# RWKV-7 layer of a two-layer hybrid: k times (1 + ka(a−1)) and k times k_k are made where the keys are projected, and y's normalisation is given out later in the recurrence

## The chip, the cores and the metric

The kernel runs on one core of a Trainium2 chip. The metric is the device time of one execution in microseconds (us), the median of several. One execution was also taken by the hardware profiler; its page and trace are the profile spoken of below.

## The reference

A two-layer model works on 1104 columns of tokens: 16 meta tokens and a prompt of 1024, which form one sequence, and eight samples of eight tokens. The width is 1024. The first layer is a gated DeltaNet mixer, the second an RWKV-7 mixer with 16 heads of 64, and only the second is touched. Its core:

```python
def rwkv_mixer(xn, S0, shift_prev, mu, w_rkvz, ..., k_k, k_a, r_k, lnx_w, lnx_b, w_o):
    ...
    r, k, v, z = rkvz[0], rkvz[1], rkvz[2], rkvz[3]
    w = -jax.nn.softplus(-(w0 + jnp.tanh(xs[4] @ w1) @ w2)) - 0.5
    a = jax.nn.sigmoid(a0 + (xs[5] @ a1) @ a2)
    kk = l2norm((k * k_k).reshape(B, T, H, N))
    k = k * (1.0 + (a - 1.0) * k_a)
    decay = jnp.exp(-jnp.exp(w))
    ...
    def step(S, inp):
        r_t, k_t, v_t, d_t, kk_t, b_t = inp
        S = (S * d_t[:, :, None, :]
             + jnp.einsum('bhvk,bhk->bhv', S, -kk_t)[..., None] * b_t[:, :, None, :]
             + v_t[..., None] * k_t[:, :, None, :])
        return S, jnp.einsum('bhvk,bhk->bhv', S, r_t)
    ...
    y = (y - mean) * lax.rsqrt(var + GN_EPS) * lnx_w.reshape(H, N) + lnx_b.reshape(H, N)
    y = y + jnp.sum(r_h * k_h * r_k, -1, keepdims=True) * v_h
    y = y.reshape(B, T, D) * jax.nn.silu(z)
    return y @ w_o, S, xn[:, -1]
```

So the raw key k is used in two ways: times k_k it gives kk, and times 1 + (a − 1)·ka it gives the key of the recurrence. `omka` below is 1 − ka, so that the factor is ka·a + omka.

## The kernel before

The 1104 columns are cut into three segments (384, 384, 336), the 1024 channels into eight tiles of 128 partitions (two heads each). A pair of tile and segment is an item; the RWKV layer has 24 of them, n = 8 × segment + tile. Matmuls of the dense projections take the weight in two float32r parts: `whi` is ScalarE's rounded copy of the loaded `wraw`, `wlo` is GpSimd's difference (line 90). The inputs `xh`, `xa`, `xc` and `xl` of a projection are split likewise, and `mixs` is the token-shift mix before the split. `d` is the PSUM tile of such a projection.

The RWKV layer runs in stages, one after the other:

1. **Keys, decay and rate** (`keys_decay_rate`, lines 1112 to 1153; 1360 to 1480 us). For each of the eight tiles, the key projection of three segments (`project`: ScalarE copies each PSUM tile into `ev`, line 1109, and SyncE stores it to DRAM, line 1110), then two second halves of low-rank products (`flora`): for the decay a sigmoid, a scan along the columns on VectorE (line 1143) and a store; for the rate a a sigmoid and a store. The three results are slices of one DRAM tensor, `cakd` (c the scanned decay, a the rate, k the raw key).
2. **Projections of r, v and z** (24 calls of `project`), between which `rwkv_inverse` is called five times (1480 to 1862 us). It loads `sldcak` (line 1221), scales kk by k_k on ScalarE (line 1251), makes the normalised kk products (lines 1257 to 1264), and solves small triangular systems (`L`, `T1n`, `invT`, `mY`, `mU`, `fL`).
3. **The recurrence** (`wave`, lines 1820 and on; 1880 to 2310 us). Items start every second step and take six chunks of 64 columns, one a step, so that up to three items are in flight; there are 58 steps. A step's chain on TensorE and ScalarE: matmuls `rX` and `rY` from the last state, ScalarE's copy `X` (line 1466), matmuls of X with the inverse (`rX<-X,rTT`, `rS<-X,rTT`), ScalarE's two `UV` copies, matmuls `rS<-UV,BT` and `rY<-UV,G` in `step_inner`, and the new state.
4. The end of the output projection and the final norm (2310 to 2351 us).

Around the chain, each step also gives out work of other items. `rwkv_front` (line 1317) prepares the next item: it loads `fldcak` (c, a, k; 576 KB, one buffer) and `fldrv`, makes the decays `fDp` and `fiD`, makes the key of the recurrence on ScalarE (`k<-fldcak,omka,pcol`, line 1342) and VectorE (line 1343), and the tile BK from it; scores `fG`, transposes `fBT` copied to `BT`, and a `bonus` follow. `rwkv_finish` (line 1518) treats an item whose six chunks are done: bn_stats, the reciprocal root `grs` and the shift `gnm` on VectorE, then six ScalarE normalisations of y in place (line 1536), and behind a `yield` the transposes `yT` and VectorE's two products into `lz` (lines 1544 and 1545; the intermediate shares a one-buffer tile, tag `k2`, with the front's key), and behind another the split into `yh` and `yl` that feeds the output projection (`zo`, `do`). `fill` gives out dense matmuls between.

What sets the order: TensorE's order in the recurrence is that of the program. The other engines' queues are ordered by the scheduler's own simulation of the program at build time; everything under `issue_after(ins)` in a step stands behind the UV copies of that step on its engine. Every engine, and SyncE with its DMA issues, executes its queue in order. In `wave`, an item's `rwkv_finish` is begun at the end of the step of its last chunk, outside the reach of the next step's `issue_after`, so the normalisations stand where the scheduler puts them. `pre` is ScalarE's decayed state for the next step, given out by `step_old` right behind UV.

Of the kernel before, what the change touches and what calls it, by code (L numbers as in the profile page):

```python
# [35 lines left out]
class Builder:  # L36
# [867 lines left out]
    ev = None  # L904
# [193 lines left out]

    def project(self, m, k, x, dst, apart=False):

        nc, t = self.nc, self.t
        w = self.load_w(self.i["rwkv_w_rkvz"][0, m][:, 128 * k:128 * k + 128])
        ps = (self.dense(w, 128, *x, s, bufs=4) for s in range(2 if m == 3 else 3)) if apart else self.dense3(w, 128, *x)
        for (c0, n), p in zip(SEGS, ps):
            f = t(self.ev, [128, 384], "ev", 3)
            if m == 3:
                self.gate(f[:, 0:n], p[:, 0:n])
            else:
                nc.scalar.copy(f[:, 0:n], p[:, 0:n])
            nc.sync.dma_start(dst[k][:, c0:c0 + n], f[:, 0:n])  # L1110

    def keys_decay_rate(self, x, hh, hl):

        nc, t, i, col = self.nc, self.t, self.i, self.pcol
        with self.tc.tile_pool(name="lora", bufs=1, reuse_waits="tile") as pool:
            z = t(pool, [128, 8, 48], "zpad")
            nc.gpsimd.memset(z, 0.0)
            for d in (self.ad, self.rd, self.vd, self.zd, self.kd):
                nc.sync.dma_start(d[:, :, NT:1152].rearrange("k p n -> p k n"), z)
# [26 lines left out]
            def dst_a(k, s, p):  # L1146
                c0, n = SEGS[s]
                f = t(self.ev, [128, 384], "ev", 3)
                self.act(f[:, 0:n], p[:, 0:n], AF.Sigmoid, bias=col["rwkv_a0"][:, k:k + 1])
                nc.sync.dma_start(self.ad[k][:, c0:c0 + n], f[:, 0:n])  # L1150
            for k in range(8):
                self.project(1, k, x, self.kd, k in (0,))
                self.lora_second(0, k, hh, w2, dst_w)
                self.lora_second(1, k, hl, w2, dst_a)
# [4 lines left out]
    def rwkv_masks(self, ap, first=False):  # L1159
# [42 lines left out]
        self.omka = t(ap, [128, 8], "omka")  # L1202
        nc.vector.tensor_scalar(self.omka, self.pcol["rwkv_k_a"], -1.0, 1.0, op0=ALU.mult, op1=ALU.add)

    def rwkv_open(self):
        self.cakd, self.rvd, self.zd = (self.dram([8, 128, n, 1152], m) for n, m in ((3, "cakd"), (2, "rvd"), (1, "zd")))
        self.csd, self.ad, self.kd = (self.cakd[:, :, x] for x in range(3))
        self.rd, self.vd = (self.rvd[:, :, x] for x in range(2))
        self.zd = self.zd[:, :, 0]
        self.ttd, self.abd = self.dram([5, 128, 1920], "ttd"), self.dram([24, 128, 768], "abd")  # L1210

    def rwkv_load(self, n, pool, tag, names):
# [4 lines left out]
        for g in names:  # L1217
            d = {"cak": self.cakd, "rv": self.rvd}[g]
            y = 1 if tag == "s" else 0
            x = t(pool, [128, y + len(g), 384], tag + "ld" + g, 1 if g == "cak" and tag == "f" else 2)  # L1220
# [18 lines left out]
    def rwkv_inverse(self, b, pool):  # L1239
# [4 lines left out]
        for q, n in enumerate(items):  # L1244
# [6 lines left out]
            self.act(kk, kk, AF.Identity, scale=self.pcol["rwkv_k_k"][:, p:p + 1])  # L1251
# [65 lines left out]
    def rwkv_front(self, p, s):  # L1317
# [11 lines left out]
        ld = self.rwkv_load(P.n, fp, "f", ("cak", "rv"))  # L1329
# [11 lines left out]
        k2 = t(fp, [128, 384], "k2", 1)  # L1341
        self.act(k2, ld["a"], AF.Identity, scale=pc("rwkv_k_a"), bias=self.omka[:, p:p + 1])
        nc.vector.tensor_tensor(k2, k2, ld["k"], op=ALU.mult)

        nc.vector.tensor_tensor(BK[:, :, 0, :], c6(k2), c6(iD), op=ALU.mult)
# [4 lines left out]
        nc.vector.scalar_tensor_tensor(pr, ld["r"], pc("rwkv_r_k"), k2, op0=ALU.mult, op1=ALU.mult)  # L1350
# [167 lines left out]
    def rwkv_finish(self, p, s, P):  # L1518
# [15 lines left out]
        nc.vector.scalar_tensor_tensor(nm, mv[:, :, 0], -1.0, rs, op0=ALU.mult, op1=ALU.mult)  # L1534
        for q in range(6):
            self.act(y(q), y(q), AF.Identity, scale=rs[:, q:q + 1], bias=nm[:, q:q + 1])
        yield
# [280 lines left out]
    def wave(self, zin, stay, last, pool):  # L1818
# [63 lines left out]
        for tau in range(-3, 55):  # L1882
# [12 lines left out]
            with self.tc.issue_after(ins) if W else ExitStack():  # L1895
                if W:
                    self.step_old(W)
                for f in begun:
                    next(f)
# [54 lines left out]
```

## Time and profile before

| | us |
|---|---|
| median of 3 runs (2350.22 to 2353.13) | 2350.88 |
| the profiled execution | 2353.39 |
| its span, first to last instruction | 2351.5 |
| TensorE busy in it | 2157.2 (92%) |
| VectorE busy | 1570.0 (67%) |
| ScalarE busy | 1298.2 (55%) |
| GpSimd busy | 922.5 (39%) |
| mean granted TensorE clock | 0.969 |

In the profile PE is TensorE's matmul side and PEld its weight loads, DVE VectorE, ACT ScalarE, POOL GpSimd and SP SyncE, which issues the DMAs. A row of a view of waits reads "waiting engine, tile and line, <- engine, tile and line waited for: us in total, times, longest". A row of a timeline reads "start, duration, engine, line, operation, out<-in, shapes, count", with the idle time before it and its releaser in brackets. A row of groups ends with "count | busy us, mean ns of one | idle us before, and what ended it". Several like instructions in a row of one engine are shown as one row with their count.

### The profile page before, as it was taken

What the parts mean: (1) busy time and instruction counts of PE and PEld (TensorE: products, weight loads), DVE (VectorE), ACT (ScalarE), POOL (GpSimd) and SP (SyncE); (2) the same over time, 40 slices, a digit from 0 to 9 for tenths busy, and PEclk for the clock granted to TensorE, in tenths of its full rate; (3) what the DMA queues carried; (4) which work ended last, traced back from release to release, by engine and by line L of the source; (5) the groups of instructions that cost most, each with busy time, mean ns of one, the idle gap of its engine ahead of it and who ended that gap; (6) DMA issues with size and microseconds to landing.
All of it is one profiled execution on the core that took longest, in us unless ns stands there. A gap on an engine that the chain in (4) does not pass through costs nothing. (4 is left out here: it accounts for less than half of the span.)

```text
span 2351.5 us, 55207 instructions
## 1 busy us (share of the span) xinstructions
PE 2157.2 (92%) x20452; PEld 1959.8 (83%) x20452; DVE 1570.0 (67%) x4176; ACT 1298.2 (55%) x3690; POOL 922.5 (39%) x1267
## 2 busy tenths in 40 slices
PE   6989999989999999999999999898888898899986
PEld 5878988889898989888999999787777876778775
DVE  6768668685857677684335842679879365667754
ACT  5455555465655645556333655746555355677763
POOL 3435334343435343444131532545324333344443
PEclk9999999999999999999999999999999999999998
DMA  4324332423333333336153154654543655577654
GB/s 114 107 67 113 84 86 79 109 63 101 91 97 96 88 101 82 93 82 206 51 147 106 47 149 167 181 167 128 172 123 94 187 141 141 174 219 229 208 167 136
DMA packets 431704, 293.36 MB, mean 125 GB/s; under 512 B 146906, under 2 KB 414283, under 8 KB 431435
## 3 DMA queue, kind: packets, MB, share of 16 engines
q1 hardware_dynamic: 431434, 289.83, 42.8%
q8 instruction: 161, 2.64, 0.5%
q14 instruction: 109, 0.89, 0.1%
HBM read 202.74 MB, written 87.00 MB: 123 GB/s over the span
## 5 line engine op out<-in xcount | busy, mean ns | idle before, releaser
L90 POOL TENSOR_TENSOR wlo<-wraw,whi 128x512 fp32r<-128x512 f32 (+2 forms) x252 | 330.9, 1315 | 370.1 <-ACT whi L86 354.6
L76 PE MATMUL d<-xc,whi 128*128 128x384 f32 (+2 forms) x910 | 258.6, 340 | 9.3 <-POOL xc L90 3.5
L86 ACT CAST whi<-wraw 128x512 fp32r<-128x512 f32 (+2 forms) x252 | 151.7, 603 | 128.1 <-PE dq L76 50.6
L415 DVE SCALAR_TENSOR_TENSOR cvy<-raw,cw,cvy 128x408 f32<-128x408 f32 (+2 forms) x288 | 178.5, 633 | 16.9 <-ACT cvy L62 15.1
L76 PEld LDWEIGHTS d<-xc,whi 128*128 128x128 f32 (+1 forms) x910 | 166.5, 189 | 15.9 <-POOL xc L90 3.8
L453 DVE TENSOR_TENSOR invT<-invT,invtmp 72x31 f32<-72x31 f32 (+31 forms) x403 | 171.5, 426 | 6.5
L451 DVE TENSOR_TENSOR invtmp<-invA,invT 72x31 f32<-72x31 f32 (+31 forms) x403 | 165.3, 410 | 12.5 <-DMA invA<-ltd 5.4
L76 PE MATMUL dz<-xc,whi 128*128 128x384 f32 (+1 forms) x480 | 149.7, 343 | 0.0
L76 PE MATMUL dv<-xc,whi 128*128 128x384 f32 (+1 forms) x480 | 146.7, 334 | 0.0
L76 PE MATMUL d<-xc,wlo 128*128 128x384 f32 (+2 forms) x428 | 141.5, 340 | 0.9 <-POOL wlo L90 0.8
L76 PE MATMUL d<-xa,whi 128*128 128x384 f32 (+3 forms) x450 | 139.3, 344 | 3.3 <-DVE xa L90 1.8
L815 POOL TENSOR_SCALAR Sb<-Sb,eglb 128x128 f32<-128x128 f32 x128 | 81.0, 651 | 89.4 <-DMA Sb<-in_state_gdn 44.4
L76 PE MATMUL dz<-xa,whi 128*128 128x384 f32 (+1 forms) x288 | 100.5, 349 | 0.0
L76 PE MATMUL dv<-xa,whi 128*128 128x384 f32 (+1 forms) x288 | 100.1, 347 | 0.1
L76 PEld LDWEIGHTS dz<-xc,whi 128*128 128x128 f32 x480 | 89.8, 192 | 0.8
L76 PEld LDWEIGHTS d<-xa,whi 128*128 128x128 f32 (+1 forms) x450 | 84.0, 191 | 7.5 <-DVE xa L90 2.4
L76 PE MATMUL d<-xa,wlo 128*128 128x384 f32 (+3 forms) x252 | 85.9, 342 | 3.8 <-POOL wlo L90 3.8
L76 PEld LDWEIGHTS dv<-xc,whi 128*128 128x128 f32 x480 | 88.5, 188 | 0.5 <-issue 0.4
L62 ACT ACTIVATE o<-rA,gcol 128x128 f32<-128x128 f32 x128 | 46.7, 373 | 73.9 <-DVE S L726 73.6
L62 ACT ACTIVATE attn<-attn,gcol 128x128 f32<-128x128 f32 x144 | 46.6, 390 | 71.8 <-POOL attn L526 71.7
L76 PE MATMUL d<-xl,whi 128*128 128x384 f32 (+1 forms) x256 | 84.2, 346 | 1.5 <-DVE xl L90 1.4
L76 PE MATMUL d<-xh,wlo 128*128 128x384 f32 (+1 forms) x256 | 83.8, 342 | 1.5 <-POOL wlo L90 1.5
(511 smaller groups left out, 7052.6 us busy)
## 6 DMA issues: line engine op xcount, KB each, us to landing
wraw<-in_gdn_w_in SPq DMA_DIRECT2D x96, 256.0 KB
wraw<-in_rwkv_w_rkvz SPq DMA_DIRECT2D x80, 256.0 KB
Sb<-in_state_gdn SPq DMA_DIRECT2D x64, 256.0 KB
sldcak<-cakd SPq DMA_DIRECT2D x24, 576.0 KB
fldcak<-cakd SPq DMA_DIRECT2D x24, 576.0 KB
cakd<-ev SPq DMA_DIRECT2D x56, 192.0 KB
wraw<-in_rwkv_w_o SPq DMA_DIRECT2D x40, 256.0 KB
E<-drow SPq DMA_DIRECT2D x24, 384.0 KB
```

The lines of the kernel that those rows point to most:

```text
L62: return self.nc.scalar.activation(out, in_, func, bias=bias, scale=scale, **kw)
L76: self.nc.tensor.matmul(out, lhsT, rhs, start=start, stop=stop)
L86: nc.scalar.copy(hi, x)
L90: e.tensor_tensor(lo, x, hi.bitcast(F32), op=ALU.subtract)
L415: nc.vector.scalar_tensor_tensor(y[:, 0:wd], raw[:, k:k + wd], cw[k], y[:, 0:wd], op0=ALU.mult, op1=ALU.add)
L451: nc.vector.tensor_tensor(tmp, A[:, j, j + 1:32].unsqueeze(2).broadcast_to([nb, n, m]), Tv[:, j, 0:m].unsqueeze(1).broadcast_to([nb, n, m] ...
L453: nc.vector.tensor_tensor(Tv[:, j + 1:32, 0:m], Tv[:, j + 1:32, 0:m], tmp, op=ALU.subtract)
L815: nc.gpsimd.tensor_scalar(Sb[:, u], Sb[:, u], self.eglb[:, hv, 4 * g + u:4 * g + u + 1], None, op0=ALU.mult)
```

## The change

Three things are altered.

- The stage of keys, decay and rate now stores k·k_k (the scaling is in ScalarE's copy out of PSUM) instead of the raw k, and besides it a fourth slice, `k2d`, with the key of the recurrence: VectorE copies the raw key from PSUM into a tile `key` (four buffers), makes ka·a + omka with a TENSOR_SCALAR, multiplies, and SyncE stores the product. `omka` is made in this stage. Per stage: 24 copies, 24 TENSOR_SCALARs, 24 products and 24 stores of up to 192 KB are new, and one store of padding zeros.
- `rwkv_inverse` loses its 24 scalings by k_k. `rwkv_front` loses its 24 ScalarE and 24 VectorE operations on the key and loads `fld2c` (the finished key and c; 384 KB, two buffers) instead of `fldcak`; the product `pr` is pinned behind the product BK in VectorE's queue.
- `rwkv_finish` has a `yield` ahead of the six normalisations and another after the fourth. `wave` takes four of them in step 2n + 6 and two in step 2n + 7, each right behind `step_old`, inside the reach of `issue_after`.

```diff
@@ -1096,12 +1096,15 @@
 
+    def projected(self, m, k, x, apart=False):
+
+        w = self.load_w(self.i["rwkv_w_rkvz"][0, m][:, 128 * k:128 * k + 128])
+        return (self.dense(w, 128, *x, s, bufs=4) for s in range(2 if m == 3 else 3)) if apart else self.dense3(w, 128, *x)
+
     def project(self, m, k, x, dst, apart=False):
 
         nc, t = self.nc, self.t
-        w = self.load_w(self.i["rwkv_w_rkvz"][0, m][:, 128 * k:128 * k + 128])
-        ps = (self.dense(w, 128, *x, s, bufs=4) for s in range(2 if m == 3 else 3)) if apart else self.dense3(w, 128, *x)
-        for (c0, n), p in zip(SEGS, ps):
+        for (c0, n), p in zip(SEGS, self.projected(m, k, x, apart)):
             f = t(self.ev, [128, 384], "ev", 3)
@@ -1115,7 +1118,9 @@
             nc.gpsimd.memset(z, 0.0)
-            for d in (self.ad, self.rd, self.vd, self.zd, self.kd):
+            omka = t(pool, [128, 8], "omka")
+            nc.vector.tensor_scalar(omka, col["rwkv_k_a"], -1.0, 1.0, op0=ALU.mult, op1=ALU.add)
+            for d in (self.ad, self.rd, self.vd, self.zd, self.kd, self.k2d):
                 nc.sync.dma_start(d[:, :, NT:1152].rearrange("k p n -> p k n"), z)
@@ -1148,8 +1153,19 @@
                 nc.sync.dma_start(self.ad[k][:, c0:c0 + n], f[:, 0:n])
+                g, kf = t(pool, [128, 384], "ev2", 2), keys.pop(0)
+                nc.vector.tensor_scalar(g[:, 0:n], f[:, 0:n], col["rwkv_k_a"][:, k:k + 1], omka[:, k:k + 1], op0=ALU.mult, op1=ALU.add)
+                nc.vector.tensor_tensor(kf[:, 0:n], g[:, 0:n], kf[:, 0:n], op=ALU.mult)
+                nc.sync.dma_start(self.k2d[k][:, c0:c0 + n], kf[:, 0:n])
+
+            keys = []
             for k in range(8):
-                self.project(1, k, x, self.kd, k in (0,))
+                for (c0, n), p in zip(SEGS, self.projected(1, k, x, k in (0,))):
+                    f = t(self.ev, [128, 384], "ev", 3)
+                    self.act(f[:, 0:n], p[:, 0:n], AF.Identity, scale=col["rwkv_k_k"][:, k:k + 1])
+                    nc.sync.dma_start(self.kd[k][:, c0:c0 + n], f[:, 0:n])
+                    keys.append(t(pool, [128, 384], "key", 4))
+                    nc.vector.tensor_copy(keys[-1][:, 0:n], p[:, 0:n])
                 self.lora_second(0, k, hh, w2, dst_w)
@@ -1199,12 +1215,10 @@
         nc.vector.tensor_scalar(self.lnb, self.pcol["rwkv_lnx_b"], 0.5, None, op0=ALU.mult)
-        self.omka = t(ap, [128, 8], "omka")
-        nc.vector.tensor_scalar(self.omka, self.pcol["rwkv_k_a"], -1.0, 1.0, op0=ALU.mult, op1=ALU.add)
 
     def rwkv_open(self):
-        self.cakd, self.rvd, self.zd = (self.dram([8, 128, n, 1152], m) for n, m in ((3, "cakd"), (2, "rvd"), (1, "zd")))
-        self.csd, self.ad, self.kd = (self.cakd[:, :, x] for x in range(3))
+        self.cakd, self.rvd, self.zd = (self.dram([8, 128, n, 1152], m) for n, m in ((4, "cakd"), (2, "rvd"), (1, "zd")))
+        self.k2d, self.csd, self.ad, self.kd = (self.cakd[:, :, x] for x in range(4))
         self.rd, self.vd = (self.rvd[:, :, x] for x in range(2))
@@ -1215,9 +1229,9 @@
         for g in names:
-            d = {"cak": self.cakd, "rv": self.rvd}[g]
+            d = {"cak": self.cakd[:, :, 1:4], "2c": self.cakd[:, :, 0:2], "rv": self.rvd}[g]
             y = 1 if tag == "s" else 0
-            x = t(pool, [128, y + len(g), 384], tag + "ld" + g, 1 if g == "cak" and tag == "f" else 2)
+            x = t(pool, [128, y + len(g), 384], tag + "ld" + g, 2)
             nc.sync.dma_start(x[:, y:], d[p][:, :, c0:c0 + 384])
@@ -1248,7 +1262,6 @@
             al, bk = ab[:, 0].rearrange("p (c k) -> p c k", k=64), ab[:, 1]
-            self.act(kk, kk, AF.Identity, scale=self.pcol["rwkv_k_k"][:, p:p + 1])
             self.act(ab[:, 0, 1:384], ld["c"][:, 0:383], AF.Exp, scale=-self.DEC)
@@ -1326,7 +1339,7 @@
             nc.sync.dma_start(P.TT.rearrange("p c k -> p (c k)"), self.ttd[(P.n + 1) // 5][:, 384 * (P.n - max(5 * ((P.n + 1) // 5) - 1, 0)):][:, 0:384])
-        ld = self.rwkv_load(P.n, fp, "f", ("cak", "rv"))
+        ld = self.rwkv_load(P.n, fp, "f", ("2c", "rv"))
         Dp, iD = self.rwkv_decays(ld, fp, "f")
@@ -1338,16 +1351,15 @@
         nc.vector.tensor_tensor(AR[:, 1], c6(ld["r"]), c6(Dp[:, 1:385]), op=ALU.mult)
-        k2 = t(fp, [128, 384], "k2", 1)
-        self.act(k2, ld["a"], AF.Identity, scale=pc("rwkv_k_a"), bias=self.omka[:, p:p + 1])
-        nc.vector.tensor_tensor(k2, k2, ld["k"], op=ALU.mult)
-
-        nc.vector.tensor_tensor(BK[:, :, 0, :], c6(k2), c6(iD), op=ALU.mult)
+        k2 = ld["2"]
+
+        last = nc.vector.tensor_tensor(BK[:, :, 0, :], c6(k2), c6(iD), op=ALU.mult).ins
         flat = lambda x: x.rearrange("p x k -> p (x k)")
...
 
         pr = t(fp, [128, 384], "pr", 1)
-        nc.vector.scalar_tensor_tensor(pr, ld["r"], pc("rwkv_r_k"), k2, op0=ALU.mult, op1=ALU.mult)
+        with self.tc.issue_after(last):
+            nc.vector.scalar_tensor_tensor(pr, ld["r"], pc("rwkv_r_k"), k2, op0=ALU.mult, op1=ALU.mult)
         ph, pl = t(fp, [128, 384], "prh", 1, F32R), t(fp, [128, 384], "prl", 1, F32R)
@@ -1532,9 +1544,11 @@
         nc.vector.scalar_tensor_tensor(nm, mv[:, :, 0], -1.0, rs, op0=ALU.mult, op1=ALU.mult)
+        yield
         for q in range(6):
             self.act(y(q), y(q), AF.Identity, scale=rs[:, q:q + 1], bias=nm[:, q:q + 1])
-        yield
+            if q in (3, 5):
+                yield
         yp = self.ps("f", 2, "yT")
@@ -1895,6 +1909,8 @@
                     self.step_old(W)
+                if 0 <= (tau - 6) // 2 < 24:
+                    next(P[(tau - 6) // 2].done)
                 for f in begun:
```

How instructions move. First ScalarE's queue in one even step of the steady recurrence (the step whose timeline the prediction reads); rX and rS are PSUM tiles of the chain, gnm and grs the shift and factor of the normalisation. Before:

```order
L1466 COPY X_28001<-rX_27998 128x192
L62 ACTIVATE y_23216<-y_23216,gnm_27974,grs_27967 128x64 x6
L62 ACTIVATE UV_23215<-rX_27998 64x3x64
L62 ACTIVATE UV_23215<-rS_28000 64x3x64
L62 ACTIVATE pre_28039<-rS_3922_23213,DC_26990 128x64
L62 ACTIVATE pre_28041<-rS_3923_23214,DC_27264 128x64
L62 ACTIVATE pre_28043<-rS_3916_23207,DC_27540 128x64
L86 CAST yh_28045<-lz_27660 128x384
L86 CAST whi_28053<-wraw_28051 128x512
L62 ACTIVATE fDp_28101<-fldcak_28097 128x384
L62 ACTIVATE fiD_28102<-fldcak_28097 128x384
L62 ACTIVATE k_4957_28113<-fldcak_28097,omka_23205,pcol_377 128x384
```

The same step now:

```order
L1478 COPY X_28062<-rX_28059 128x192
L62 ACTIVATE UV_23336<-rX_28059 64x3x64
L62 ACTIVATE UV_23336<-rS_28061 64x3x64
L62 ACTIVATE pre_28100<-rS_3970_23334,DC_27067 128x64
L62 ACTIVATE pre_28102<-rS_3971_23335,DC_27338 128x64
L62 ACTIVATE pre_28104<-rS_3964_23328,DC_27611 128x64
L62 ACTIVATE y_23337<-y_23337,gnm_28041,grs_28034 128x64 x4
L86 CAST yh_28110<-lz_27730 128x384
L86 CAST whi_28118<-wraw_28116 128x512
L62 ACTIVATE fDp_28166<-fld2c_28162 128x384
L62 ACTIVATE fiD_28167<-fld2c_28162 128x384
L1528 COPY y_23337<-rY_28060 128x192
```

The row of six y stood between X and UV; four of them now stand behind `pre`, and `k` is gone from behind `fiD`. The other two are in the next step, again behind `pre`:

```order
L62 ACTIVATE UV_23336<-rX_28179 64x3x64
L62 ACTIVATE UV_23336<-rS_28181 64x3x64
L62 ACTIVATE pre_28220<-rS_3970_23334,DC_27067 128x64
L62 ACTIVATE pre_28222<-rS_3971_23335,DC_27338 128x64
L62 ACTIVATE pre_28224<-rS_3964_23328,DC_27611 128x64
L62 ACTIVATE y_23337<-y_23337,gnm_28041,grs_28034 128x64 x2
L86 CAST prh_28230<-pr_28228 128x384
L86 CAST whi_28241<-wraw_28239 128x512
```

In that step `prh` stood right behind `pre` before.

Second, GpSimd's queue at the end of the stage of keys, decay and rate, where it makes its share of the mixes (line 90, outputs xc, xl, xa) for the first projection of the next stage, and clears the tiles of the inverse (MEMSET). Before:

```order
L90 TENSOR_TENSOR xa_103<-mixs_18230,xa_103 128x384
L90 TENSOR_TENSOR xc_107<-mixs_18240,xc_107 128x384
L1164 MEMSET m_strs_3190_18150 128x64
L1181 MEMSET hones_18160 128x32
L1183 MEMSET rk_3193_18162 128x160
L1186 MEMSET sGD_18164 128x32x8
L442 MEMSET invT_18617 128x1024
L1303 MEMSET sTD_18165 32x32x32 x2
L1169 AFFINE_SELECT m_strs_3190_18150<-m_strs_3190_18150 64x64 x2
L90 TENSOR_TENSOR xc_107<-mixs_18250,xc_107 128x384
L1172 AFFINE_SELECT m_strs_3190_18150<-m_strs_3190_18150 64x64 x2
L90 TENSOR_TENSOR xl_2814_15536<-mixs_18260,xh_2813_15535 128x384
```

Now:

```order
L90 TENSOR_TENSOR wlo_18994<-wraw_18991,whi_18993 128x512
L90 TENSOR_TENSOR xc_107<-mixs_18387,xc_107 128x384
L1145 MEMSET ev_18257 128x48
L90 TENSOR_TENSOR xc_107<-mixs_18397,xc_107 128x384
L90 TENSOR_TENSOR xl_2814_15536<-mixs_18407,xh_2813_15535 128x384
L1180 MEMSET m_strs_3239_18297 128x64
L1197 MEMSET hones_18307 128x32
L1199 MEMSET rk_3242_18309 128x160
L1202 MEMSET sGD_18311 128x32x8
L1185 AFFINE_SELECT m_strs_3239_18297<-m_strs_3239_18297 64x64 x2
L90 TENSOR_TENSOR xa_103<-mixs_18417,xa_103 128x336
L442 MEMSET invT_18760 128x1024
```

One xc, the xl and one xa that stood behind the clearing now stand ahead of it, or behind fewer of its rows; the clearing of invT comes later among them.

Third, VectorE's queue at the same place; line 1025 makes mixes, line 90 splits them, line 1143 (1148 now) is the scan, and `ev` and `key` belong to the last tile. Before:

```order
L1143 SCALAR_TENSOR_TENSOR ev_3177_18108<-sm_2969_17015,ev_18106 128x384
L1025 SCALAR_TENSOR_TENSOR mixs_18230<-xb_2707_14511,pcol_377,mixs_18230 128x384
L1025 SCALAR_TENSOR_TENSOR mixs_18235<-xb_2708_14512,pcol_377,mixs_18235 128x384
L1143 SCALAR_TENSOR_TENSOR ev_3180_18116<-sm_2970_17016,ev_18114 128x384
L90 TENSOR_TENSOR xa_103<-mixs_18183,xa_103 128x384
L1143 SCALAR_TENSOR_TENSOR ev_3183_18125<-sm_2970_17016,ev_18122 128x384
L90 TENSOR_TENSOR xa_103<-mixs_18235,xa_103 128x384
L1025 SCALAR_TENSOR_TENSOR mixs_18240<-xb_2709_14513,pcol_377,mixs_18240 128x384
L1025 SCALAR_TENSOR_TENSOR mixs_18245<-xb_2710_14514,pcol_377,mixs_18245 128x384
L1025 SCALAR_TENSOR_TENSOR mixs_18250<-xb_2711_14515,pcol_377,mixs_18250 128x384
```

Now:

```order
L1168 COPY key_18226<-d_18148 128x384
L1158 TENSOR_TENSOR key_18079<-ev_3205_18132,key_18079 128x336
L1168 COPY key_18231<-d_18149 128x384
L1025 SCALAR_TENSOR_TENSOR mixs_18387<-xb_2709_14513,pcol_377,mixs_18387 128x384
L1168 COPY key_18236<-d_18150 128x336
L1148 SCALAR_TENSOR_TENSOR ev_3223_18243<-sm_2970_17018,ev_18241 128x384
L1148 SCALAR_TENSOR_TENSOR ev_3226_18251<-sm_2971_17019,ev_18249 128x384
L90 TENSOR_TENSOR xa_103<-mixs_18330,xa_103 128x384
L1025 SCALAR_TENSOR_TENSOR mixs_18392<-xb_2710_14514,pcol_377,mixs_18392 128x384
L90 TENSOR_TENSOR xa_103<-mixs_18382,xa_103 128x384
L1148 SCALAR_TENSOR_TENSOR ev_3229_18260<-sm_2971_17019,ev_18257 128x384
L1025 SCALAR_TENSOR_TENSOR mixs_18397<-xb_2711_14515,pcol_377,mixs_18397 128x384
```

The last tile's three copies into `key` stand among the scans and mixes; its three TENSOR_SCALARs and products (lines 1157 and 1158) follow between the next mixes, up to ten rows further down. In the recurrence itself TensorE's order is the same before and now.

## The prediction

> **What bounds the kernel now.** I read the totals by engine, then a table of the stages that the change touches, then TensorE's waits stage by stage, then single steps. The profiled run took 2353.39 us: a span of 2351.5 and 1.9 around it. TensorE is busy 2157.2 us of the span, so what it waits for is what can be won. The table has one stage to a row; columns: window, its length, busy us (and instructions) of TensorE, its weight loads, VectorE, ScalarE and GpSimd, the granted clock, DMA share and GB/s.
>
> ```profile
> 1360.00:1466.00 106.00, 103.93 (x616) 102.52 (x615) 33.00 (x43) 53.78 (x106) 27.64 (x33) 1.00 0.54 169
> 1466.00:1480.00 14.00, 10.98 (x57) 9.20 (x55) 10.94 (x15) 12.64 (x28) 7.36 (x11) 1.00 0.51 162
> 1480.00:1494.00 14.00, 8.95 (x38) 7.45 (x38) 8.60 (x15) 11.49 (x25) 9.46 (x19) 0.76 0.92 219
> 1562.00:1842.00 280.00, 244.99 (x3152) 221.55 (x3153) 218.24 (x414) 157.60 (x387) 107.73 (x117) 0.95 0.43 130
> 2040.00:2310.00 270.00, 243.97 (x3801) 207.64 (x3793) 178.47 (x629) 190.26 (x558) 115.30 (x121) 1.00 0.69 207
> ```
>
> The first row is the stage of keys, decay and rate: TensorE idles 2.1 us of 106. Then come the turn to the projections of r, v and z (two rows), most of the inverses, and the later recurrence, where TensorE idles 26.0 us at full clock. TensorE's waits in the whole recurrence (us in total, times, longest):
>
> ```profile
> PE rS L80 <- ACT UV L62: 11.0, 14, 1.1
> PE drsw L76 <- DVE xss L1588: 9.7, 6, 3.3
> PE rX L80 <- ACT X L1466: 3.7, 9, 0.6
> PE fG L76 <- ACT BT L1385: 3.5, 4, 1.2
> PE fG L76 <- DVE k L1544: 1.3, 2, 0.7
> PE zo L76 <- POOL yl L90: 1.1, 2, 0.6
> ```
>
> The longest entry is the wait for UV, ScalarE's copy from which the next step's state and output are made. One steady even step shows why; first ScalarE (start, duration), then TensorE:
>
> ```profile
> 2156.72 0.32 ACT L1466 COPY X<-rX 128x192 f32<-128x192 f32 x1 [1.37 <-PE rX L80]
> 2157.88 2.10 ACT L62 ACTIVATE y<-y,gnm,grs 128x64 f32<-128x64 f32 x6 [0.85 <-DVE gnm L1534]
> 2160.01 0.33 ACT L62 ACTIVATE UV<-rX 64x192 f32<-64x192 f32 x1
> 2163.07 0.69 ACT L62 ACTIVATE k<-fldcak,omka,pcol 128x384 f32<-128x384 f32 x1
> 2164.38 0.34 ACT L1466 COPY X<-rX 128x192 f32<-128x192 f32 x1
> ...
> 2166.00 0.33 ACT L62 ACTIVATE UV<-rX 64x192 f32<-64x192 f32 x1 [1.28 <-PE rS L80]
> ```
>
> ```profile
> 2157.83 0.22 PE L80 MATMUL rS<-X,rTT 64*64 64x64 f32 x1
> ...
> 2159.30 0.34 PE L76 MATMUL fbonus<-prl,bones 128*128 128x384 f32 x1
> 2160.60 0.57 PE L80 MATMUL rS<-UV,BT 128*64 128x64 f32 x12 [0.97 <-ACT UV L62]
> ```
>
> What UV reads was ready at 2158.05. ScalarE had just begun six normalisations of y; they end at 2159.98 and UV starts behind them. TensorE's other work covers up to 2159.64, the rest is the 0.97.
>
> **The change part by part.**
>
> *Normalising y later.* Six ScalarE instructions, 2.10 us, leave the place between X and UV: four go behind UV and `pre` of the same step, two behind `pre` of the next. UV can then start near 2158.1, its two halves of 0.33 us end before 2158.8, and TensorE's next matmul is ready at 2159.64. The whole 0.97 goes, and so do the like gaps: **−11.0 us** (14 waits). The ends: −11.0 if nothing else is late, −5.5 if ScalarE hands half of it on.
>
> What is late next? From UV to the next X copy ScalarE took 2164.38 − 2160.01 = 4.37 us, `k` included. With four normalisations (4 × 0.35) and without `k` it is 4.37 + 1.40 − 0.69 = 5.08 us. UV starts earlier by about 1.9, the step shortens by 0.97, so X is reached about 0.9 − 0.7 = 0.2 us sooner against TensorE than before. In the odd step two normalisations add 0.70 where ScalarE idled 1.28 before UV. So these moves cost nothing by themselves; without that cover they cost up to 0.7 a step. What consumes y sits one stage further down: `yh` and `yl` feed the output matmuls, and I book three waits like the quoted two of `yl` (1.1/2 each): **+1.5**.
>
> *The front without its two k operations.* ScalarE's `k` goes (24 × 0.695) and VectorE's product goes (24 × 0.813):
>
> ```profile
> L62 ACT ACTIVATE k<-fldcak,omka,pcol 128x384 f32<-128x384 f32 x22 | 15.3, 695 | 0.0
> L1343 DVE TENSOR_TENSOR k<-k,fldcak 128x384 f32<-128x384 f32 x22 | 17.9, 813 | 0.1
> ```
>
> Neither has a TensorE wait in its own name. The gain is in what stands behind them: the X copies (3.7), the BT copies (3.5) and `k` of line 1544 (1.3), whose buffer no longer serves the front as well. Bounds: 0, and all three, −8.5. ScalarE's load of the even step hardly falls (0.2 us), so I take the lower part: **−2** (−1 of X, −1 of the other two). The loads shrink from 576 to 384 KB and get a second buffer: that can only bring them earlier.
>
> *The stage of keys, decay and rate.* ScalarE's copies become scaled ones: 24 × (0.58 − 0.48) = 2.4 us by the first two rows below. VectorE gets 72 more operations; the copies and TENSOR_SCALARs I price as the lone product of 0.56 us quoted further down: 72 × 0.56 = 40 us. SyncE's queue gets 24 more stores and one of padding.
>
> ```profile
> L62 ACT ACTIVATE ev<-flora,pcol 128x384 f32<-128x384 f32 x32 | 18.2, 580 | 16.4 <-PE flora L76 11.8 <-DMA cakd<-ev 4.2
> L1109 ACT COPY ev<-d 128x384 f32<-128x384 f32 x18 | 8.4, 478 | 5.5 <-DMA cakd<-ev 5.5
> ...
> L1143 DVE TENSOR_TENSOR_SCAN ev<-sm,ev 128x384 f32<-128x384 f32 x24 | 22.6, 953 | 53.7 <-ACT ev L62 52.4 <-DMA cakd<-ev 1.2
> ```
>
> ```profile
> ACT ev L1109 <- DMA cakd<-ev: 7.5, 6, 2.1
> ```
>
> ```profile
> SPq L1144 <- DVE ev L1143: 26.9, 20, 3.0
> ```
>
> VectorE has 73 idle us here, ScalarE 52; 40 and 2.4 fit. I book **0**. The price if the cover is gone: a key's PSUM bank is now read by two engines, and the second one's queue is in order. Its copy can stand behind a scan (0.95) or wait for one of four key buffers whose store has not landed; stores held ScalarE 7.5 us in 6 waits (up to 2.1), with no TensorE wait behind most of them. SyncE issues in order too: the new store waits for VectorE's product, and the weight loads behind it wait along, as 20 waits on the scan do already. Bounds: 0, and 2.0 us in each of eight projections, +16.
>
> *The turn to the projections.* TensorE's waits there, then the engines around them:
>
> ```profile
> PE d L76 <- POOL xc L90: 3.5, 1, 3.5
> PE d L76 <- DVE xa L90: 1.8, 2, 1.2
> PE d L76 <- ACT xa L86: 1.2, 1, 1.2
> ```
>
> ```profile
> 1478.08 0.95 POOL L442 MEMSET invT<- 128x1024 f32 x1
> 1479.09 1.95 POOL L1303 MEMSET sTD<- 32x1024 f32 x2
> ...
> 1481.72 1.01 POOL L90 TENSOR_TENSOR xc<-mixs,xc 128x384 fp32r<-128x384 f32 x1
> ```
>
> ```profile
> 1482.00:1490.00 8.00, 4.95 (x14) 3.71 (x15) 4.00 (x8) 7.97 (x17) 5.83 (x13) 0.61 1.07 212
> ```
>
> In the new order GpSimd's mixes of this segment stand ahead of those memsets (2.90 us) and ScalarE, busy 7.97 of 8 us, loses some of its scalings of kk. Against that, the last project's nine new VectorE operations stand among the mixes. Upper end: nine times 0.56 = +5. Lower end: the 3.5 gone and the slow clock with it; at 0.61, 4.95 × 0.39 = 1.9, so −5.4. I take **−1**, since both queues feed the same matmuls and either can be last.
>
> ```profile
> 1476.74 1.25 DVE L90 TENSOR_TENSOR xc<-mixs,xc 128x384 fp32r<-128x384 f32 x1
> ...
> 1480.31 0.56 DVE L90 TENSOR_TENSOR xl<-mixs,xh 128x384 fp32r<-128x384 f32 x1
> ```
>
> ```profile
> 1476.25 1.32 POOL L90 TENSOR_TENSOR xc<-mixs,xc 128x384 fp32r<-128x384 f32 x1 [2.89 <-ACT xc L86]
> ```
>
> The same VectorE product took 0.56 us alone and 1.25 us over a GpSimd product. A price by this: 0.69 more for the three new products of the last project is +2.1, inside the +5. The Trainium skill's page "SBUF — State Buffer" (section "SBUF: two separate sides") says that a VectorE operation with two SBUF inputs and a GpSimd operation that reads SBUF share a port pair as an exclusive lock; the two rows agree. By that rule all 24 new products could be held up, 24 × 0.69 = 17 us of VectorE, which still fits into its idle time.
>
> *The inverses.* 24 ScalarE operations of 0.615 us go, but TensorE's longest waits are on VectorE's chain:
>
> ```profile
> L62 ACT ACTIVATE sldcak<-sldcak,pcol 128x384 f32<-128x384 f32 x22 | 13.5, 615 | 57.8 <-DMA sldcak<-cakd 30.0 <-issue 9.7 <-DVE sldcak L1264 8.5
> ```
>
> ```profile
> PE mY L76 <- DVE T1n L1304: 10.1, 5, 3.4
> PE fL L76 <- DVE sldcak L1264: 7.6, 5, 2.2
> ```
>
> The load itself is what the scaling waited for most, and it stays. Line 1264 may come up to 0.6 us earlier in each of its 5 waits (−3), and a reshuffled order may cost as much. **0**, between −4 and +4.
>
> *The sum:* −11.0 + 1.5 − 2 + 0 − 1 + 0 = −12.5, so 2353.39 − 12.5 = 2340.9. The median of the three runs, 2350.88, lies 2.5 below the profiled run: 2338.4, rounded to **2339 us**. The sample steps' 9.7 us of `drsw` wait for `xss`, which the change doesn't touch: 0.
>
> **The rivals.** Differences go on the median.
> - *A new wait takes half of it.* y's four normalisations delay X or BT, or `yl` becomes late oftener than I booked: −11 turns into −5.5 and the front's −2 into 0, with +1.5 and −1: −5, **2346 us**. For it: only 0.2 us of ScalarE margin gained in the even step. Against it: fG runs between X's copy and its use. Chance 0.17.
> - *The turn also loses its wait and slow clock.* −12.5 − 4.4 more (−5.4 for −1), **2334 us**. For it: the memsets leave the way. Against it: VectorE's nine additions. Chance 0.13. On the Trainium skill's page "TensorE: Matmul & The Clock Gate" (section "What's actually happening") an idle window of about 3.4 us gives half rate; the trace agrees, 3.48 us of idle stand ahead of the stretch at 0.61.
> - *The keys' stage becomes the bound.* From the point where the stores of k or VectorE's queue hold a PSUM bank longer than the other bank lasts, each of eight projections stalls for one landing, +16, and VectorE, late by then, brings the turn to its upper end, +5 for −1: −12.5 + 16 + 6 = +9.5, **2360 us**. For it: four buffers for three tiles a project, and ScalarE's waits on stores today. Against: 73 us of idle VectorE. Chance 0.13.
> - *The gaps only move.* If TensorE's fill work, not UV, paces the pairs of steps, −11 becomes about 0 and the sum −1.5: **2349 us**. For it: TensorE is busy 90% there. Against: its work and order stay the same, so a gap removed must shorten the step. Chance 0.07.
>
> **How the numbers follow.** Forecast 0.50, rivals as given. Below 0.2% (4.7 us) a measurement of this kernel can't tell from no change: faster is under 2346.2, slower over 2355.6. The forecast, the larger gain and a little over half of the half gain, which lies at the bound, count as faster, less 0.02 for a forecast that slips: 0.70. The rest of the half gain, the moved gaps and that 0.02 make 0.17; slower is the third rival, 0.13. The range: at the top up to 2355, so that little but the third rival is left out; at the bottom 2326, the sum with the −4 of the inverses, the −5.4 of the turn and about half of what the front leaves on the table (−4). The forecast's own range is 2331 to 2346.
>
> **What would show it.** Right: the wait `rS <- UV` gone or under 2 us; the window of the later recurrence some 10 us shorter with the same TensorE busy time; ScalarE's normalisations behind `pre`; the X and BT waits not above 7.2 together. Wrong: the X, BT or yl waits up by more than 5; TensorE's idle time in the keys' stage above 2.1 by several us with waits on VectorE's key copies, on `ev` or on `wlo`; or a turn longer than its 28 us.

## The result, and the profile after

The changed kernel takes 2344.38 us (median of 13 runs, 2333.26 to 2352.16) against 2352.54 (13 runs, 2340.53 to 2359.38): a ratio of 0.9959, 95% interval 0.9942 to 0.9977, where 2339 against 2350.88 was forecast (0.995). Its profiled run took 2352.16 us (span 2350.4), the longest of the 13, so the two spans say nothing: the unchanged DeltaNet layer alone, up to the last matmul frb<-dg, took 1340.2 us in the profile before and 1347.3 in this one. Stretches are compared instead: from there to the first matmul rX<-X,rTT (keys to inverses), and the recurrence itself, counted in 52 steps (0 to 51) by the first rX<-X,rTT of each.

| stretch, us | before | before, second profile | changed | changed, second profile |
|---|---|---|---|---|
| last frb<-dg to step 0 | 542.8 | 544.0 | 547.2 | 544.2 |
| steps 0 to 16 (with the samples) | 151.2 | 148.3 | 148.3 | 147.3 |
| steps 16 to 44 (steady pairs) | 219.8 | 219.5 | 209.8 | 208.6 |
| steps 44 to 51 | 52.5 | 53.9 | 52.4 | 53.0 |

A steady pair is an even step and the odd one behind it; these pairs give 10 us. TensorE's waits in the recurrence after (window 1880 to 2310 us, as in the prediction):

```profile
PE drsw L76 <- DVE xss L1602: 8.1, 5, 3.6
PE fG L76 <- ACT BT L1397: 7.4, 5, 5.3
PE zz L76 <- DVE zst L984: 3.7, 2, 2.8
PE rX L80 <- ACT X L1478: 3.0, 7, 0.6
...
PE rX L80 <- DMA rTT<-ttd: 2.3, 3, 1.3
...
PE zo L76 <- POOL yl L90: 1.6, 3, 0.6
...
PE rS L80 <- ACT UV L62: 0.4, 1, 0.4
```

The wait for UV fell from 11.0 to 0.4 us. One even step (24), first ScalarE, then TensorE:

```profile
2102.61 0.33 ACT L62 ACTIVATE UV<-rX 64x192 f32<-64x192 f32 x1 [1.04 <-PE rS L80]
2102.84 0.31 ACT L62 ACTIVATE UV<-rS 64x192 f32<-64x192 f32 x1
2103.91 1.42 ACT L62 ACTIVATE y<-y,gnm,grs 128x64 f32<-128x64 f32 x4
2107.12 0.32 ACT L1528 COPY y<-rY 128x192 f32<-128x192 f32 x1
2107.34 0.48 ACT L1397 COPY BT<-fBT 128x384 f32<-128x384 f32 x1
2107.71 0.34 ACT L1478 COPY X<-rX 128x192 f32<-128x192 f32 x1
```

```profile
2104.09 0.57 PE L80 MATMUL rS<-UV,BT 128*64 128x64 f32 x12
...
2107.51 1.29 PE L76 MATMUL fG<-AR,BK 64*128 64x128 f32 x12
```

`rS` now follows without a gap. So far the prediction looks right in number and cause. The experiments show that the cause isn't.

### The profile page after: what moved, and what is told of

It is laid out like the page before. It is cut to its first block, busy times and chain, and to the rows that moved or that the text cites. A ratio compares the mean times of both kernels' runs of the same rounds, so it can differ in the third digit from the quotient of the medians.

```text
span 2350.4 us, 55277 instructions
## 1 busy us (share of the span) xinstructions
PE 2161.4 (92%) x20452; PEld 1966.9 (84%) x20452; DVE 1603.1 (68%) x4224; ACT 1272.2 (54%) x3642; POOL 926.3 (39%) x1267
## 5 line engine op out<-in xcount | busy, mean ns | idle before, releaser
L76 PE MATMUL d<-xc,whi 128*128 128x384 f32 (+2 forms) x910 | 263.7, 346 | 7.0 <-DVE key L1168 2.2
L86 ACT CAST whi<-wraw 128x512 fp32r<-128x512 f32 (+2 forms) x252 | 151.7, 604 | 123.8 <-PE dq L76 50.5
L415 DVE SCALAR_TENSOR_TENSOR cvy<-raw,cw,cvy 128x408 f32<-128x408 f32 (+2 forms) x288 | 179.6, 637 | 17.1 <-ACT cvy L62 15.3
L76 PE MATMUL d<-xc,wlo 128*128 128x384 f32 (+2 forms) x428 | 145.5, 346 | 0.5 <-POOL wlo L90 0.5
```

What stands on the lines that cost most here:

```text
L76: self.nc.tensor.matmul(out, lhsT, rhs, start=start, stop=stop)
L86: nc.scalar.copy(hi, x)
L415: nc.vector.scalar_tensor_tensor(y[:, 0:wd], raw[:, k:k + wd], cw[k], y[:, 0:wd], op0=ALU.mult, op1=ALU.add)
```

## The experiments

**The two parts apart, the loads first, and before once more.** `y_only` is the kernel before with the three edits of `rwkv_finish` and `wave`; `keys_only` is the changed kernel without them. `lw_first`:

```diff
+            wr = t(pool, [128, 2, D], "lw2")
+            for q in (0, 64):
+                nc.sync.dma_start(wr[q:q + 64, 0], i["rwkv_w2"][0])
+                nc.sync.dma_start(wr[q:q + 64, 1], i["rwkv_a2"][0])
             z = t(pool, [128, 8, 48], "zpad")
...
-            wr = t(pool, [128, 2, D], "lw2")
-            for q in (0, 64):
-                nc.sync.dma_start(wr[q:q + 64, 0], i["rwkv_w2"][0])
-                nc.sync.dma_start(wr[q:q + 64, 1], i["rwkv_a2"][0])
```

> The kernel before with only the later normalisation of y (keys, inverse and front as before). Theory A (the whole gain is the UV gap): the wait of rS for UV under 1 us of 11.0, the span from the first to the last matmul rX<-X,rTT 412 us (423.5 before, 410.5 after), the time 10 to 11 us under the kernel before (-0.45%). Rival B (the front without its two k operations carries half of the recurrence's gain): that span not under 417 us, the time only 5 to 6 us under before.

> The changed kernel with y normalised as before (only the keys' part of the change). Theory A: the wait for UV stays near 11 us, the span of rX<-X,rTT 421 to 424 us, the stretch from the last frb<-dg to the first rX<-X,rTT 547 us (542.8 before, 547.3 after), so the time 2 to 4 us over before. Rival B: the span of rX<-X,rTT near 417, the time 3 to 5 us under before. Rival C (the 4.5 us between the stretches of before and after is only a difference from execution to execution): that stretch near 543, the time within 2 us of before.

> The changed kernel with the four loads of the low-rank weights written ahead of the padding stores, so that SyncE issues them some 5 us sooner. Theory A (SyncE's new order, two key stores and all the padding ahead of these loads, starts the stage late and leaves TensorE at the slow clock): TensorE's wait for lw2h gone, the last frb<-dg to the first flora 37 to 38 us (37.4 before, 39.8 after), the time 3 us under that of the changed kernel, 13 us under before (-0.55%). Rival C: the same -0.4% as the changed kernel.

> The kernel before, unaltered, once more under the profiler, to see how far a stretch differs from execution to execution. Theory A: the stretch from the last frb<-dg to the first rX<-X,rTT within 2 us of 542.8, that of rX<-X,rTT within 2 us of 423.5. Rival C: one of them off by 4 us or more.

| kernel | ratio to before (95%) | to step 0 | 0 to 16 | 16 to 44 | 0 to 51 |
|---|---|---|---|---|---|
| before / again | | 542.8 / 544.0 | 151.2 / 148.3 | 219.8 / 219.5 | 423.4 / 421.7 |
| y_only | 0.9993 (0.9973 to 1.0014) | 542.8 | 154.1 | 217.0 | 426.6 |
| keys_only | 0.9939 (0.9918 to 0.9960) | 547.1 | 144.8 | 213.4 | 410.4 |
| lw_first | 0.9915 (0.9890 to 0.9940) | 541.0 | 147.9 | 210.3 | 411.4 |

On the recurrence theories A and B are both wrong, and C finds nothing in the second profile of before. With y moved alone the UV wait is gone (0.4 us left) and the time stays; with the keys' part alone the UV wait stays at 10.1 us and the recurrence is 11 to 13 us shorter. The even step 28 shows why: BT's copy on ScalarE and the fG group on TensorE, in before, `y_only` and `keys_only`.

```profile
2133.32 0.48 ACT L1385 COPY BT<-fBT 128x384 f32<-128x384 f32 x1
...
2133.36 1.43 PE L76 MATMUL fG<-AR,BK 64*128 64x128 f32 x12
```

```profile
2124.88 0.49 ACT L1385 COPY BT<-fBT 128x384 f32<-128x384 f32 x1
...
2124.49 0.48 PE L76 MATMUL fG<-AR,BK 64*128 64x128 f32 x2
2125.41 0.93 PE L76 MATMUL fG<-AR,BK 64*128 64x128 f32 x10 [0.44 <-ACT BT L1385]
```

```profile
2117.53 0.57 PE L80 MATMUL rS<-UV,BT 128*64 128x64 f32 x12 [1.11 <-ACT UV L62]
...
2120.33 0.49 ACT L1397 COPY BT<-fBT 128x384 f32<-128x384 f32 x1
...
2120.95 0.94 PE L76 MATMUL fG<-AR,BK 64*128 64x128 f32 x12
```

Undisturbed, the twelve fG matmuls take 0.94 us (`keys_only`). In before the row is 1.43 long: ten of the twelve stand behind BT's copy (end 2133.80), whose source is a PSUM tile of the two-buffer tag "f" that fG needs next. The view merges a group of like matmuls, so this half microsecond counts as busy time and is in no list of waits. In `y_only` the same wait is long enough to be listed, with its 0.44 us.

So the even step ends 0.92 us after BT's copy, or with TensorE's own chain, whichever is later. Counted from the step's start, BT's copy ends at 7.12 before (step 8.04), at 6.40 with y moved (7.32), at 5.81 with both (6.72). With the keys' part alone it ends at 6.55, no longer last, and TensorE's chain with its UV gap of 1.11 sets 7.55. In `late_y24` (described below), where two normalisations fewer stand ahead of it, the copy ends at 5.15, fG takes its 0.94 again, and the step is 6.38 long:

```profile
2109.33 0.49 ACT L1397 COPY BT<-fBT 128x384 f32<-128x384 f32 x1
...
2110.18 0.94 PE L76 MATMUL fG<-AR,BK 64*128 64x128 f32 x12
```

Moving y alone does therefore shorten an undisturbed pair: from 15.27 to 14.77 us at steps 28 and 29, and by 0.36 to 0.59 in the pairs that begin at 22, 26, 28 and 30. Over the fourteen pairs from 16 to 44 less than half of that is left (2.8 us), in part because in three even steps TensorE waited for the load of the inverse, which in the first profile of before it never did:

```profile
PE rX L80 <- DMA rTT<-ttd: 3.4, 3, 2.2
```

In that stretch this wait is 2.3 to 3.4 us in the four profiles with y moved for all items, 0 to 2.4 in the eight with y as before. Whether the move makes the load late was not tried.

`lw_first`: the loads of the low-rank weights had become late. SyncE's queue at the start of the stage, after and before:

```profile
1368.09 3.89 SPq L1166 DMA_DIRECT2D cakd<-ev  x2
1372.08 0.49 SPq L1132 DMA_DIRECT2D lw<-in_rwkv_w  x1
1372.66 0.54 SPq L1124 DMA_DIRECT2D cakd<-zpad  x1
1373.25 2.05 SPq L1124 DMA_DIRECT2D rvd<-zpad  x2
...
1379.78 0.60 SPq L1133 DMA_DIRECT2D lw<-in_rwkv_a  x1
```

```profile
1362.55 1.02 SPq L1119 DMA_DIRECT2D cakd<-zpad  x1
1363.68 0.96 SPq L1127 DMA_DIRECT2D lw<-in_rwkv_w  x1
...
1366.21 0.60 SPq L1128 DMA_DIRECT2D lw<-in_rwkv_a  x1
```

From the last frb<-dg the last of these loads was issued 26.0 us on before and 32.4 after. The padding stood ahead of the loads before as well; new are the two key stores, 3.89 us long because they wait for ScalarE, ahead of both. With the loads ahead of the padding the last of them is issued at 26.5, TensorE's wait for `lw2h` (1.1) is gone, the first flora comes 34.4 us after frb<-dg (39.8 changed, 37.4 before), more than expected, and the stretch to step 0 is 6.2 us shorter than in the first profile of the changed kernel, 3.2 than in its second.

**Which of the front's operations it was.** `no_act_k` leaves ScalarE's operation out, `no_dve_k` VectorE's product, `load_two` only gives the front's load its second buffer; `act_k_pin` is `no_act_k` with two pins. The edits, in this order:

```diff
-        self.act(k2, ld["a"], AF.Identity, scale=pc("rwkv_k_a"), bias=self.omka[:, p:p + 1])
-        nc.vector.tensor_tensor(k2, k2, ld["k"], op=ALU.mult)
+        nc.vector.tensor_tensor(k2, ld["a"], ld["k"], op=ALU.mult)
...
-        nc.vector.tensor_tensor(k2, k2, ld["k"], op=ALU.mult)
...
-            x = t(pool, [128, y + len(g), 384], tag + "ld" + g, 1 if g == "cak" and tag == "f" else 2)
+            x = t(pool, [128, y + len(g), 384], tag + "ld" + g, 2)
...
+        with self.tc.issue_after(ar):
+            nc.vector.tensor_tensor(k2, ld["a"], ld["k"], op=ALU.mult)
...
+        with self.tc.issue_after(last):
             nc.vector.scalar_tensor_tensor(pr, ld["r"], pc("rwkv_r_k"), k2, op0=ALU.mult, op1=ALU.mult)
```

> The kernel before, with ScalarE's operation on the key left out of the front (the key of the recurrence is then a times k without ka and omka, so outputs that depend on it differ); VectorE's product, the loads and y as before. Steps are counted by the first matmul rX<-X,rTT of each, 0 to 51. Theory D (in the even step ScalarE's queue from gnm to X, not the UV gap, paces the pair; 0.69 us of it goes): the 14 pairs from step 16 to 44 take 213 to 215 us (219.8 before, 213.4 with the keys' part alone), the wait for UV stays at 10 us, the time 5 to 6 us under before or more. Rival E (the smaller load with its second buffer, or VectorE's product, made the gain): those pairs stay at 219 us, the time as before.

> The kernel before, with VectorE's product with the key left out of the front (the key of the recurrence is then ka a + omka alone, so outputs that depend on it differ); ScalarE's queue, the loads and y as before. Theory D: the pairs from step 16 to 44 stay at 219 us; steps 0 to 16, where VectorE makes the samples' operands, take 146 to 148 us (151.2 and 148.3 before, 144.8 with the keys' part alone). Rival E: the pairs come down to 213 to 215 us.

> As no_act_k (ScalarE's operation on the key left out of the front, so outputs that depend on the key differ), but with VectorE's product pinned behind that of AR and pr behind that of BK, so that neither stands in VectorE's queue ahead of G. Theory D (ScalarE's queue paces the even step, and the earlier 22 us were VectorE's new order): steps 16 to 44 in 213 to 215 us (219.8 before, 213.4 with the keys' part alone), the wait for UV still 10 us, the wait of fbonus for G gone; steps 0 to 16 in 143 to 148 us. The time 6 to 10 us under before. Rival E (the gain comes with the smaller load and its second buffer): steps 16 to 44 in 219 us.

> The kernel before with nothing but two buffers for the front's load of c, a and k. Theory D: steps 16 to 44 in 219 us, steps 0 to 16 in 148 to 151 us, the time as before. Rival E: steps 16 to 44 in 214 us, or steps 0 to 16 in 145 us or less.

| kernel | ratio to before (95%) | 0 to 16 | 16 to 44 | even step 28 | odd step 29 |
|---|---|---|---|---|---|
| before | | 151.2 | 219.8 | 8.04 | 7.23 |
| no_act_k | 1.0138 (1.0101 to 1.0175) | 158.9 | 235.0 | 8.67 | 7.22 |
| no_dve_k | 0.9994 (0.9976 to 1.0011) | 151.7 | 220.9 | 8.03 | 7.23 |
| load_two | 0.9989 (0.9970 to 1.0007) | 157.1 | 219.1 | 8.03 | 7.21 |
| act_k_pin | 0.9980 (0.9959 to 1.0001) | 146.9 | 219.7 | 7.26 | 7.97 |
| keys_only | 0.9939 (0.9918 to 0.9960) | 144.8 | 213.4 | 7.55 | 7.19 |

No single piece makes the gain. The second buffer, half of rival E, falls with `load_two`; its other half, the smaller load, was not tried alone. Steps 0 to 16 missed their range in `no_dve_k` (151.7 for 146 to 148) and `load_two` (157.1 for 148 to 151), at 20.5 and 30.7 us of half-rate clock in them (see the steps with the samples, below). Of the stretches 16 to 44 that of `no_act_k` holds 17.1 us of it, those of `no_dve_k` and `act_k_pin` 3.4 each. `no_act_k` missed: VectorE's queue was reordered, the product and `pr` got ahead of G and waited there for their loads. The waits of `no_act_k`, then of the later recurrence of `act_k_pin`:

```profile
PE fbonus L76 <- DVE G L1375: 15.5, 10, 3.0
```

```profile
PE rS L80 <- ACT UV L62: 7.3, 12, 1.0
PE fVT L73 <- DVE G L1377: 3.3, 7, 0.5
```

With the pins the even step falls by 0.78 us, as theory D has it, and the odd one grows by 0.74: G, behind VectorE's product, is late for fVT there. VectorE at the end of step 28, in before (which starts at 2126.68) and in `act_k_pin` (2123.14):

```profile
2133.11 1.10 DVE L1343 TENSOR_TENSOR k<-k,fldcak 128x384 f32<-128x384 f32 x1
...
2135.54 0.98 DVE L1376 TENSOR_TENSOR G<-fG,gm 128x384 f32<-128x384 f32 x2
```

```profile
2128.75 1.63 DVE L1343 TENSOR_TENSOR k<-fldcak 128x384 f32<-128x384 f32 x1
...
2132.17 0.99 DVE L1377 TENSOR_TENSOR G<-fG,gm 128x384 f32<-128x384 f32 x2
```

Counted from the step's start, VectorE comes to G at 8.86 in before and at 9.03 here, although the next step begins 0.78 sooner; in `keys_only`, without the product, it is 8.48. D's total (213 to 215 us) was wrong because two queues pace the pair, ScalarE's the even step and VectorE's next behind it. Of the kernels with y as before only `keys_only` shortens the pairs (15.27 to 14.74 us at step 28). It has both operations out, but also the smaller load and the pin of `pr`; that the pin keeps `no_act_k`'s trouble away was not tried by itself.

**Versions of the change.** `keys_lw` is `keys_only` with the loads first. `late_y` is `lw_first` with the later y for segments 1 and 2 alone (`if s:` ahead of the new yields); `late_y24` splits the six two and four:

```diff
-            if s and q in (3, 5):
+            if s and q in (1, 5):
```

> The changed kernel with y normalised as before and the four loads of the low-rank weights ahead of the padding stores. Theory D with A's order of the loads: steps 0 to 51 at 410.5 us as with the keys' part alone, the last frb<-dg to the first rX<-X,rTT 541 us, the time 1.0% under before, at or below that with y moved as well (0.9915). A rival (y's move is worth its 3 us in the steady pairs overall): 3 us or more above that kernel.

> As keys_lw, but y's normalisation given out later for the items of the second and third segment alone, those whose steps hold no samples. Theory D (y's move costs 3 us in steps 0 to 16 and saves 3 to 4 in the pairs from 16 to 44): steps 0 to 16 in 145 us, 16 to 44 in 210 us, steps 0 to 51 in 407 us, the time 1.1% under before. A rival (the 3 us in the samples' steps are only a difference between executions): steps 0 to 16 at 148 us, the time as with y moved for all items.

> As late_y, but two of the six normalisations in the even step and four in the odd one. Theory D (the end of ScalarE's BT copy bounds the even step as long as fG waits for it inside its group): without 0.70 us ahead of it in ScalarE's queue BT ends before fG needs it, the even step falls from 6.74 to about 6.4 us; the odd step, where ScalarE has idle time before UV, grows from 7.35-7.46 by 0.1 to 0.5. Steps 0 to 51 in 405 to 409 us (407.0 with four and two), the time as with four and two, within 0.2%. A rival (BT has nothing to do with it): the even step stays at 6.7 us.

> The changed kernel, unaltered, once more under the profiler. If the stretches are the kernel's own and not the execution's: the last frb<-dg to the first rX<-X,rTT 547 us within 2, steps 0 to 16 in 148 us within 2, steps 16 to 44 in 210 us within 1, even steps of 6.72 and 7.60 and odd ones of 7.34 and 7.45 us. What comes before the last frb<-dg may differ by 10 us.

| kernel | ratio to before (95%) | to step 0 | 0 to 16 | 16 to 44 | 0 to 51 |
|---|---|---|---|---|---|
| keys_lw | 0.9943 (0.9924 to 0.9963) | 539.5 | 142.8 | 213.8 | 411.5 |
| late_y | 0.9902 (0.9878 to 0.9927) | 539.3 | 144.1 | 209.5 | 406.8 |
| late_y24 | 0.9930 (0.9909 to 0.9950) | 539.6 | 145.5 | 212.9 | 411.8 |

`late_y` came out within 1 us of what was expected on every stretch and has the lowest time of all, 0.6% under the changed kernel's ratio, with intervals that don't overlap; against `lw_first` (0.9915) they do, so by the time alone its y is not shown to be better. In `late_y24` the even step fell to 6.37 us as theory D said, but the odd one grew from 7.35 to 8.00, by more than the 0.5 allowed: four normalisations don't fit there, and steps 0 to 51 missed their 405 to 409. `keys_lw` missed its 1.0%, although its stretches came out as expected: its time shows nothing of the 6 us that its profile has over that of `keys_only`. Its runs scatter from 2326.79 to 2344.53, and its interval is 0.2% (4.7 us) wide to each side; what else hides them stays open. `after_again` repeats the steps to 0.01 us in most places, but its stretch to step 0 is 544.2, not 547: of the 4.5 us that rival C put down to the execution, 3 were.

**The steps with the samples.** Steps 0 to 16 of before, `y_only`, `keys_only` and the changed kernel, one row each (columns as in the prediction):

```profile
1883.00:2034.20 151.20, 131.93 (x1818) 107.74 (x1817) 95.24 (x312) 82.08 (x230) 53.23 (x62) 0.92 0.51 141
```

```profile
1871.96:2026.03 154.07, 133.22 (x1817) 108.46 (x1817) 94.33 (x309) 81.53 (x229) 52.37 (x62) 0.91 0.51 142
```

```profile
1880.49:2025.27 144.78, 124.26 (x1818) 101.47 (x1816) 91.96 (x301) 78.10 (x221) 54.40 (x62) 0.96 0.50 139
```

```profile
1894.56:2042.82 148.26, 128.76 (x1818) 103.93 (x1816) 93.06 (x301) 77.26 (x221) 54.28 (x62) 0.94 0.49 135
```

The same number of matmuls, at a granted clock of 0.92, 0.91, 0.96 and 0.94; the order of the times is the order of the clocks. The trace's record of the clock has it in stretches of half rate, multiples of 3.41 us: 24.0, 27.3, 10.2 and 17.1 us here, 13.7 in the second profile of before and 20.5 in `act_k_pin` (146.9 us). The four profiles with the keys' part and y not moved in these steps have 6.8 to 13.7 us of it, the three with the keys' part and y moved for all 13.7 to 17.1, the seven others 13.7 to 30.7. So both edits may act here through the clock; with so few profiles of each, and before itself at 24.0 and 13.7, that is not separated from chance.

## Why the prediction was right and where it was wrong

The sign came out, and the number near enough; the main term's cause did not, so that the number is right was luck. The recurrence takes the same 410.4 us in `keys_only` and in the first profile of the changed kernel: y's move, booked at −11, is worth nothing in it on top of the keys' part, and the keys' part, booked at −2 there, makes the 11.3 to 13.0 us. (The sum's 2338.4 also rounds to 2338, not 2339; nothing hangs on it.) By its steps:

- **y later, −11.0.** The wait went, the time did not: in the steady pairs y alone is worth 219.8 − 217.0 = 2.8 us (after the 3.4 of waits for the inverse), on the keys' part 3.6 (213.4 to 209.8), and steps 0 to 16 are longer by as much in these profiles (144.8 to 148.3). The failed step is the sum "From UV to the next X copy", 4.37 us before and 5.08 after, with its end "So these moves cost nothing by themselves": I followed the queue to X, and BT's copy, the one just ahead of X, was what TensorE needed first. The even step fell by 0.72 us and not by 0.97. The four normalisations that left the UV gap went into that stretch. The rival "a new wait takes half of it" named BT, and its counter-argument, that fG runs meanwhile, was the mistake: fG was itself the waiting group. The odd step also paid, 0.23 us for its two (7.23 to 7.46 at step 29), where I had booked nothing. The sign that I had named for this, the X and BT waits above 7.2 together, was no help: the list after has 10.4, but 5.3 of it is one wait ahead of step 0 (before, the like wait of 4.7 lies ahead of the window), and what BT costs in the steps is mostly inside fG.
- **The front, −2.** Mis-sized from the same cause: the keys' part alone shortens steps 16 to 44 by 6.4 us, and steps 0 to 16 by 3.5 to 6.4. ScalarE's load "hardly falls" only with y moved into it; what counts is the load ahead of BT.
- **The stage of keys, 0.** The cover held for VectorE: the stage's new products took 15.2 us in all (10.6 and 4.6 below). Alone they take 0.56 (384 columns) and 0.50 (336), 13.0 in all, so 2.2 us were lost, and three products that ran over one of GpSimd (1.53, 1.26 and 1.11 us) make all of it; six others overlapped with GpSimd and lost nothing. By the Trainium skill's rule ("SBUF — State Buffer", "SBUF: two separate sides") I had worked out 17 us as the most.

```profile
L1158 DVE TENSOR_TENSOR key<-ev,key 128x384 f32<-128x384 f32 x16 | 10.6, 661 | 0.5
...
L1158 DVE TENSOR_TENSOR key<-ev,key 128x336 f32<-128x336 f32 x8 | 4.6, 576 | 0.0
```

  A key's copy did hold TensorE twice (3.1 us), not in all eight projections. What I missed is the head of SyncE's queue; loads first is worth 6.3 us there (means of the profiles, next item).
- **The turn, −1, and the inverses, 0.** Not measured apart, since TensorE's order changes in both. At the turn the wait for GpSimd's `xc`, 2.5 to 3.5 us in all seven profiles of before's stages, is gone in all seven of the new ones, as the second rival hoped; in five of these a wait of 1.5 to 1.7 for VectorE's `xl` stands in its place. The whole stretch to step 0 is 544.0 us in the mean of the seven profiles with before's stages (542.8 to 547.3), 546.2 in three with the new ones (544.2 to 547.2), 539.9 in four with the loads first (539.3 to 541.0). The first step, 2.2, is within the spread, the second, 6.3, isn't.
- **yl, +1.5.** zo's and do's waits for `yl` went from 2.1 to 2.9: +0.8, about half of what was booked.

## What to carry to other kernels

A wait's size in the list is not what its removal is worth: moving work out of one gap of an in-order queue puts it ahead of the next thing that the same queue owes, so find every consumer on that queue down to the end of the step, not only the one on the chain. A group of like instructions that takes longer than its undisturbed twin (1.43 against 0.94 us) hides a wait that no list of waits has. And where a stage gets new stores, look at what its DMA queue issued first before.

## What was not expected of the hardware

Executions of the changed kernel spread by 19 us (2333 to 2352), and the profiles of all these kernels hold 112 to 166 us of half-rate clock within their spans. The Trainium skill's "TensorE: Matmul & The Clock Gate" ("What's actually happening") gives the window as about 3.4 us; the records agree, 3.41 us. In most steady pairs there is none of it, and apart from single waits (the one for the inverse above) their steps repeat to some 0.01 us, so they tell kernels apart where whole times can't.
